# Hybrid encoder block on one core: entry norm with its scalars in PSUM, the triangular inverse in two halves, the mixing shift moved to the project stage

## The chip, the cores and the metric

The kernel runs on 1 core of one Trainium2 chip. The time is the device time of one launch in microseconds (us): the median of three runs. The profile is one further execution, recorded by the hardware profiler. The engines are named as in the profile: PE (matmuls), PEld (its weight loads), DVE (vector), ACT (scalar), POOL (GpSimd), SP (which only issues DMAs here). Each engine works through its own queue in order; an instruction that has to wait holds all behind it on that engine.

## The reference

The input x is 1024 rows (tokens) of 1024 numbers, all in float32. What the changed stages compute:

```python
h = _layer_norm(x, ln_in_w, ln_in_b)            # (x - mean) * rsqrt(var + 1e-5) * w + b, by row
proj = h @ w_in[l]                              # IN_COLS = 1696 (RWKV-7) + 2056 (attention)
...
prev = jnp.pad(p, ((0, 0), (1, 0), (0, 0)))[:, :-1]
p = p + mu * (prev - p)                         # the mixing shift, v is columns 1024 to 1535
...
state = state * wt + sa * bt + vt * kt          # RWKV-7, one step for each token, 8 heads
```

Behind it come the attention of the other 8 heads, the output projection with a norm, a router that picks 4 of 32 experts, the experts (two matrix products with a gated activation between) and a last norm. None of that is touched.

## The kernel before

Tokens are worked in 8 blocks of 128 rows. A product of float32 quality is made of three products of a rounded type: hi x whi, hi x wlo, lo x whi, where hi is the rounded operand and lo what the rounding left.

The stages, in the order of the program:

- **Entry** (the first `with` block of `hybrid_kernel`, lines 161 to 197). For each block: load x, `layer_norm2` (DVE: two `bn_stats`, `bn_aggr`, then the inverse root by three Newton steps on tiles of 128x1 in `rsqrt_steps`, lines 280 to 294; ACT: x times rstd plus a bias, line 318; DVE: times w, line 319; POOL: plus b, line 320). PE turns h (eight transposes, line 182), ACT rounds it to hi (184), DVE takes lo (185), and PE multiplies it by the 512 columns of the v weights in two halves of 24 products each (`ts_mm`, lines 154 to 156). The product v is stored to DRAM (`vraw_d`), read back shifted by one row, mixed with mu by three POOL instructions (194 to 196) and stored as `vp_d`.
- **Project** (`rw_project`): 20 groups of 24 `ws_mm` products of 512 columns on PE for the other RWKV columns, in 4 pairs of heads, each with a long chain on DVE and ACT whose results come back to PE as a few small products (lines 420, 436, 458).
- **Prep** (`rw_prep`) and **attention projections** (`fx_project`), interleaved. `rw_prep` has two loops over 16 chunks of 64 tokens. The first forms the chunk's matrices and keeps their triangular part in `lq`. Then the 16x16 diagonal blocks are inverted: `lq` goes to DRAM (`lq_d`, line 542), comes back with one block per partition and slot (`un`, 544), DVE runs 15 rounds of forward substitution (line 555 four times and line 557 once in each), the result goes to DRAM (`tr_d`, 560) and back (`cmp`, shown as trc, 563). The second loop masks it (577) and completes the inverse with products on PE (583). `fx_project` makes 64 groups of 24 products; each group's result is copied by ACT (476), squared by ACT (479) and summed by DVE (480) in a buffer of which there is one.
- **Scan, attention, output projection, experts, last norm**: unchanged.

Outside the parts that are marked as scheduled by hand, the order on each engine is set when the program is built, by a scheduler that simulates the engines; the program's text sets only what depends on what. So an edit in one stage can move instructions in others. SP issues nearly all loads, in one queue.

Of the kernel before, what the change touches and what calls it, by code (L numbers as in the profile page):

```python
# [74 lines left out]
def hybrid_kernel(ctx: ExitStack, tc: tile.TileContext, A, out):  # L75
# [84 lines left out]
    with tc.tile_pool(name="lnp", bufs=2) as lp:  # L160
        lw = lp.tile([P, D], FT, name="lw", bufs=1)
        lb = lp.tile([P, D], FT, name="lb", bufs=1)
        mub = lp.tile([P, 512], FT, name="mub", bufs=1)
        zr = lp.tile([1, 512], FT, name="zr", bufs=1)
        ve.memset(zr, 0.0)
        sp.dma_start(vraw_d[0:1, :], zr)
        wv = []
        for t in range(NT):
            x = lp.tile([P, D], FT, name="x", bufs=3)
            sp.dma_start(x, A["x"][t * P:(t + 1) * P, :])  # L170
            if t == 0:
# [4 lines left out]
                sp.dma_start(mub, bcast(A["mu_v"], 512))
            h = layer_norm2(nc, lp, x, lw, lb, name="h")
            sp.dma_start(h_d[t * P:(t + 1) * P, :], h)
            for g in range(2):
# [5 lines left out]
                ve.tensor_tensor(lo[dst], ps, f32(hi[dst]), op=OP.subtract)  # L185
            v = lp.tile([P, 512], FT, name="v")
            for j in range(2):
                ps = pa.tile([P, 512], FT, name="mm", bufs=2)[:, :256]
                ts_mm(ps, *wv[j], t)
                ac.copy(v[:, 256 * j:256 * j + 256], ps)  # L190
            sp.dma_start(vraw_d[1 + t * P:1 + (t + 1) * P, :], v)
            d = lp.tile([P, 512], FT, name="vd")
            sp.dma_start(d, vraw_d[t * P:(t + 1) * P, :])
            gp.tensor_tensor(d, d, v, op=OP.subtract)
            gp.tensor_tensor(d, d, mub, op=OP.mult)
            gp.tensor_tensor(d, d, v, op=OP.add)
            sp.dma_start(vp_d[t * P:(t + 1) * P, :], d)

# [1401 lines left out]
```

## Time and profile before

| | |
|---|---|
| Median of 3 runs | 2535.25 us (2532.88 to 2537.62) |
| Profiled execution, its own time | 2537.38 us |
| Span of the profile | 2535.7 us |
| PE busy | 2377.8 us (94%) |
| DVE busy | 1873.3 us (74%) |
| ACT busy | 1323.9 us (52%) |
| POOL busy | 406.8 us (16%) |

A share of busy time is an average over stages with different limits, so the rows below are taken by stage. Times in them are microseconds from the start of the span unless marked ns. Profiled matmuls overlap, so that the start of one to the start of the next, and not the length of one, is the pace.

### The profile page before, as it was taken

How to read it: one execution, taken by the hardware profiler on the slowest of the kernel's cores; microseconds unless marked ns; L12 is line 12 of the kernel's file. 1: busy time of each engine (PE TensorE's matmuls, PEld its weight loads, DVE VectorE, ACT ScalarE, POOL GpSimd, SP SyncE). 2: the span in 40 equal slices, each digit the busy share in tenths (PEclk: the TensorE clock that was granted, in tenths of full speed). 3: DMA queues.
4: the chain of work that ended last, by engine and by line, in shares of the span. 5: the costliest groups of instructions: out<-in, count | busy, mean ns of one | idle time of the engine just before them, and what ended most of it. 6: DMA issues, size and time to landing. Idle time of an engine off the chain costs nothing. (4 is left out here: it accounts for less than half of the span.)

```text
span 2535.7 us, 37299 instructions
## 1 busy us (share of the span) xinstructions
PE 2377.8 (94%) x14105; PEld 1810.4 (71%) x14105; DVE 1873.3 (74%) x2806; ACT 1323.9 (52%) x1610; POOL 406.8 (16%) x370
## 2 busy tenths in 40 slices
PE   5999998989988997789999999999999999999996
PEld 5778998977776765567666767766676676667772
DVE  8367334376887687678878978878897887888884
ACT  2354432364344443346666656666666666566661
POOL 4400211122121111001111101111110111111112
PEclk9999999999999998789999999999999999999998
DMA  6323874127455524569778878977887897788973
GB/s 231 135 74 137 267 228 86 61 80 242 146 191 184 195 76 182 191 208 346 291 281 306 313 299 322 339 292 293 301 332 291 312 336 293 292 302 343 345 291 134
DMA packets 184441, 606.62 MB, mean 239 GB/s; under 512 B 69881, under 2 KB 95609, under 8 KB 130626
## 3 DMA queue, kind: packets, MB, share of 16 engines
q1 hardware_dynamic: 155810, 525.24, 54.6%
q0 software_dynamic: 17456, 65.02, 9.4%
q10 hardware_dynamic: 10992, 13.93, 1.8%
q8 instruction: 113, 1.85, 0.3%
q14 instruction: 70, 0.57, 0.1%
HBM read 518.64 MB, written 85.50 MB: 238 GB/s over the span
## 5 line engine op out<-in xcount | busy, mean ns | idle before, releaser
L1196 DVE TENSOR_TENSOR wl<-raw,wh 128x2048 fp32r<-128x2048 f32 x384 | 873.2, 2288 | 147.0 <-ACT wh L1193 145.9
L1193 ACT CAST wh<-raw 128x2048 fp32r<-128x2048 f32 x381 | 725.9, 1915 | 187.0 <-PE o L1275 67.3
L1219 PE MATMUL h<-wh,xh 128*128 128x512 f32 x1024 | 300.5, 415 | 4.1 <-ACT wh L1193 4.1
L1219 PE MATMUL h<-wl,xh 128*128 128x512 f32 x1024 | 283.0, 398 | 0.2 <-DVE wl L1196 0.2
L1219 PE MATMUL h<-wh,xl 128*128 128x512 f32 x1024 | 281.1, 396 | 0.0
L1219 PEld LDWEIGHTS h<-wl,xh 128*128 128x128 f32 x1024 | 194.2, 190 | 47.8 <-DVE wl L1196 1.0
L1219 PEld LDWEIGHTS h<-wh,xl 128*128 128x128 f32 x1024 | 193.4, 189 | 47.0
L1219 PEld LDWEIGHTS h<-wh,xh 128*128 128x128 f32 x1024 | 184.6, 190 | 42.0 <-ACT wh L1193 4.5
L156 PE MATMUL mm<-whi,hT_lo 128*128 128x256 f32 x640 | 187.3, 294 | 9.5 <-DVE hT_lo L185 5.3
L154 PE MATMUL mm<-whi,hT_hi 128*128 128x256 f32 x640 | 187.7, 294 | 5.5 <-ACT sq L479 3.9
L155 PE MATMUL mm<-wlo,hT_hi 128*128 128x256 f32 x640 | 186.5, 292 | 0.0
L1014 POOL DMA_INDIRECT xg<-h_d,idx x32 | 49.7, 1552 | 777.4 <-PE o L1275 680.5
L1275 PE MATMUL o<-wh,ah 128*128 128x512 f32 x512 | 167.5, 408 | 1.7 <-ACT o L1283 1.7
L1275 PE MATMUL o<-wl,ah 128*128 128x512 f32 x512 | 160.8, 395 | 0.0
L1275 PE MATMUL o<-wh,al 128*128 128x512 f32 x512 | 160.7, 395 | 0.0
L156 PEld LDWEIGHTS mm<-whi,hT_lo 128*128 128x128 f32 x640 | 127.0, 199 | 11.4 <-DVE hT_lo L185 6.5
L154 PEld LDWEIGHTS mm<-whi,hT_hi 128*128 128x128 f32 x640 | 127.0, 198 | 8.8 <-ACT sq L479 4.3
L1213 PE MATMUL ex<-raw,xt 128*32 128x512 f32 x1152 | 132.2, 600 | 0.0
L155 PEld LDWEIGHTS mm<-wlo,hT_hi 128*128 128x128 f32 x640 | 127.1, 199 | 0.0
L1275 PEld LDWEIGHTS o<-wh,ah 128*128 128x128 f32 x512 | 91.0, 188 | 35.2 <-issue 10.9
L1275 PEld LDWEIGHTS o<-wh,al 128*128 128x128 f32 x512 | 96.2, 188 | 23.2
L1275 PEld LDWEIGHTS o<-wl,ah 128*128 128x128 f32 x512 | 96.2, 188 | 23.1
(431 smaller groups left out, 4094.8 us busy)
## 6 DMA issues: line engine op xcount, KB each, us to landing
raw<-w SPq DMA_DIRECT2D x384, 1024.0 KB
pks<-pk_d SPq DMA_DIRECT2D x16, 1152.0 KB
pk_d<-pk POOLq DMA_DIRECT2D x16, 896.0 KB, 5.6
h_d<-h SPq DMA_DIRECT2D x17, 512.0 KB
raw<-w_fx ACTq DMA_DIRECT2D x8, 1024.0 KB
fx_d<-fraw POOLq DMA_DIRECT2D x64, 128.0 KB, 2.8
qkvo<-fx_d SPq DMA_DIRECT2D x32, 256.0 KB
x<-x SPq DMA_DIRECT2D x8, 512.0 KB
```

The lines of the kernel that those rows point to most:

```text
L154: pe.matmul(ps, hi[:, k, n], whi[:, k], start=(k == 0), stop=False)
L155: pe.matmul(ps, hi[:, k, n], wlo[:, k], start=False, stop=False)
L156: pe.matmul(ps, lo[:, k, n], whi[:, k], start=False, stop=(k == KD - 1))
L1014: gp.indirect_dma_start(out=x, out_offset=None, in_=h1_d, in_offset=bass.IndirectOffsetOnAxis(ap=idx[0:m, i:i + 1], axis=0))
L1193: ac.copy(highs[i], raw)
L1196: ve.tensor_tensor(l, raw, f32(h), op=OP.subtract)
L1213: pe.matmul(px[32 * c:32 * c + 32], xt[:, k], raw[:, m], start=False, stop=(k == KD - 1))
L1219: pe.matmul(ps[:, c], x[:, k], w[:, m], start=False, stop=z)
L1275: pe.matmul(po[:, c], x[:, k], w[:, m], start=(k == 0 and x is ah and w is h), stop=z)
```

## The change

Three edits:

1. **Entry.** The order of the entry stage is written out by hand (`tc.manual_schedule()`), with the norm of block t + 2 ahead of the products of block t. The new `layer_norm_in` keeps mean, variance and the two Newton temporaries in PSUM (tile `cps`), drops the last multiplication by -1/8192 and puts that factor into w: a product of a column of -1/8192 with the row w writes w, repeated over 128 partitions, into two PSUM tiles (named qk), and DVE's multiplication by w reads it there, in two halves. POOL's addition of b goes in two halves too. The third load of w, 128 rows from DRAM, is gone; the DVE takes the wlo of the second v weight, which POOL took before.
2. **Mixing shift.** The load of mu, the reading back of v, the three POOL instructions and the store move from the entry into `rw_project`. POOL now loads both v and its shifted rows (two DMAs, line 473 of the new kernel) and stores the result (484), all from its own queue; before, SP issued these DMAs.
3. **Inverse.** `invert(g)` does the inversion for 64 of the 128 partitions, once after chunk 7 and once after chunk 15. All its tiles are set up ahead of the first loop. Each half has 15 rounds with the same number of DVE instructions as the whole had. `un` and `tr_d` are moved in eight DMAs of 8 partitions where each was one.

```diff
 
     def load_w(src, ncols=256, queue=ac, low=ve):
+        raw = fetch_w(src, ncols, queue)
+        return split_w(raw, ncols, low)
+    def fetch_w(src, ncols=256, queue=ac):
         raw = st.tile([P, KD, 256], FT, name="raw")
         queue.dma_start(raw[:, :, :ncols], src)
+        return raw
+    def split_w(raw, ncols=256, low=ve):
         whi = st.tile([P, KD, 256], FR, name="whi")
         wlo = st.tile([P, KD, 256], FR, name="wlo")
...
-        lw = lp.tile([P, D], FT, name="lw", bufs=1)
         lb = lp.tile([P, D], FT, name="lb", bufs=1)
-        mub = lp.tile([P, 512], FT, name="mub", bufs=1)
         zr = lp.tile([1, 512], FT, name="zr", bufs=1)
         ve.memset(zr, 0.0)
-        sp.dma_start(vraw_d[0:1, :], zr)
-        wv = []
-        for t in range(NT):
-            x = lp.tile([P, D], FT, name="x", bufs=3)
-            sp.dma_start(x, A["x"][t * P:(t + 1) * P, :])
-            if t == 0:
-                wv.append(load_w(A["w_v"][0], queue=sp))
-                sp.dma_start(lw, bcast(A["ln_in_w"], D))
-                sp.dma_start(lb, bcast(A["ln_in_b"], D))
-                wv.append(load_w(A["w_v"][1], queue=sp, low=gp))
-                sp.dma_start(mub, bcast(A["mu_v"], 512))
-            h = layer_norm2(nc, lp, x, lw, lb, name="h")
-            sp.dma_start(h_d[t * P:(t + 1) * P, :], h)
+        lrow = lp.tile([1, D], FT, name="lrow", bufs=1)
+        fac = lp.tile([1, P], FT, name="fac", bufs=1)
+        ve.memset(fac, -1.0 / 8192.0)
+        lw = [pq.tile([P, 512], FT, name="qk", bufs=3) for _ in range(2)]
+        cps = pa.tile([P, NT, 8], FT, name="av")
+        xs = []
+        def load_x():
+            t = len(xs)
+            xs.append(lp.tile([P, D], FT, name="x", bufs=4))
+            sp.dma_start(xs[t], A["x"][t * P:(t + 1) * P, :])
+        hs = {}
+        def turn(t):
...
+                hs[t, g] = lambda dst=dst, ps=ps: ve.tensor_tensor(lo[dst], ps, f32(hi[dst]), op=OP.subtract)
+        def low(t):
+            for g in range(2):
+                hs.pop((t, g))()
+        def values(t, j, v):
+            ps = pa.tile([P, 512], FT, name="mm", bufs=2)[:, :256]
+            ts_mm(ps, *wv[j], t)
+            ac.copy(v[:, 256 * j:256 * j + 256], ps)
+        def norm(t):
+            hs[t], r, nm = layer_norm_in(nc, lp, xs[t], cps[:, t])
+            ac.activation(hs[t], xs[t], AF.Identity, bias=nm, scale=r)
+        def weigh(t):
+            h = hs[t]
+            for c in range(2):
+                q = slice(512 * c, 512 * c + 512)
+                ve.tensor_tensor(h[:, q], h[:, q], lw[c], op=OP.mult)
+                gp.tensor_tensor(h[:, q], h[:, q], lb[:, q], op=OP.add)
+            sp.dma_start(h_d[t * P:(t + 1) * P, :], h)
+        with tc.manual_schedule():
+            load_x()
+            sp.dma_start(lrow, A["ln_in_w"][None, :])
+            for c in range(2):
+                pe.matmul(lw[c], fac, lrow[:, 512 * c:512 * c + 512], start=True, stop=True)
+            rv = [fetch_w(A["w_v"][0], queue=sp)]
+            sp.dma_start(lb, bcast(A["ln_in_b"], D))
+            load_x()
+            rv.append(fetch_w(A["w_v"][1], queue=sp))
+            load_x()
+            sp.dma_start(vraw_d[0:1, :], zr)
+            norm(0)
+            weigh(0)
+            wv = [split_w(rv[0])]
+            norm(1)
+            turn(0)
+            low(0)
+            weigh(1)
+            wv.append(split_w(rv[1]))
+            for t in range(NT):
+                if t + 3 < NT:
+                    load_x()
+                if t + 2 < NT:
+                    norm(t + 2)
+                v = lp.tile([P, 512], FT, name="v")
+                values(t, 0, v)
+                if t + 1 < NT:
+                    turn(t + 1)
+                    low(t + 1)
+                if t + 2 < NT:
+                    weigh(t + 2)
+                values(t, 1, v)
+                sp.dma_start(vraw_d[1 + t * P:1 + (t + 1) * P, :], v)
...
+def layer_norm_in(nc, pool, x, ps):
+    ve = nc.vector
+    stt = pool.tile([P, 2, 6], FT, name="ln_st")
+    for c in range(2):
+        ve.bn_stats(stt[:, c], x[:, 512 * c:512 * c + 512])
+    mean, var, a, s = ps[:, 0:1], ps[:, 1:2], ps[:, 2:3], ps[:, 3:4]
+    ve.bn_aggr(ps[:, 0:2], stt)
+    ve.tensor_scalar(a, var, LN_EPS, None, op0=OP.add)
+    r = pool.tile([P, 1], FT, name="ln_r")
+    ve.tensor_scalar(r.bitcast(I32), a.bitcast(I32), -0.5, 1597463007.0, op0=OP.mult, op1=OP.add)
+    for c in (3.0, 12.0, 768.0):
+        ve.scalar_tensor_tensor(s, a, r, r, op0=OP.mult, op1=OP.mult)
+        ve.scalar_tensor_tensor(r, s, c, r, op0=OP.subtract, op1=OP.mult)
+    nm = pool.tile([P, 1], FT, name="ln_nm")
+    ve.scalar_tensor_tensor(nm, mean, -1.0, r, op0=OP.mult, op1=OP.mult)
+    return pool.tile([P, D], FT, name="h", bufs=3), r, nm
...
+        mub = ew.tile([P, 512], FT, name="mub")
+        sp.dma_start(mub, L["bcast"](A["mu_v"], 512))
+        vs = {}
+        def fetch(t):
+            vs[t] = [ew.tile([P, 512], FT, name=n, bufs=2) for n in ("vs", "vd")]
+            for x, o in zip(vs[t], (1, 0)):
+                gp.dma_start(x, vraw_d[o + t * P:o + (t + 1) * P, :])
+        def shift(t):
+            if t == 0:
+                fetch(0)
+            if t + 1 < NT:
+                fetch(t + 1)
+            v, d = vs.pop(t)
+            gp.tensor_tensor(d, d, v, op=OP.subtract)
+            gp.tensor_tensor(d, d, mub, op=OP.mult)
+            gp.tensor_tensor(d, d, v, op=OP.add)
+            gp.dma_start(vp_d[t * P:(t + 1) * P, :], d)
...
             wnext = load_w(A["w_rk"][p + 1] if p + 1 < NP else A["w_fx"][0])
+            for t in (2 * p, 2 * p + 1):
+                shift(t)
...
+    NG = NU // 2
+    def invert(g):
+        p, us = slice(64 * g, 64 * g + 64), slice(NG * g, NG * g + NG)
+        for b in range(8):
+            q = slice(16 * b, 16 * b + 16)
+            o = 16 * (b % 4)
+            sp.dma_start(lq_d[b, us].rearrange("u s t -> s u t"), lq[q, us, o:o + 16])
+        for b in range(8):
+            sp.dma_start(un[64 * g + 8 * b:64 * g + 8 * b + 8].rearrange("p u s t -> p (u s t)"),
+                         lq_d[b, us].rearrange("(x u) s t -> x (u s t)", u=4))
+        T, R = tr[p, :, :, 0], tr[p, :, :, 1]
+        for i in range(1, 16):
+            for u in range(4):
+                ve.tensor_tensor(tm[p, u, :i * i].rearrange("p (k j) -> p k j", j=i), T[:, u, 0:i, 0:i].rearrange("p j k -> p k j"),
+                                 un[p, u, None, 0:i, i].to_broadcast([64, i, i]), op=OP.mult)
+            ve.tensor_reduce(T[:, :, i, 0:i], tm[p, :, :i * i].rearrange("p u (k j) -> p u k j", j=i), axis=AX.X, op=OP.add)
+        for u in range(4):
+            ve.tensor_copy(R[:, u], T[:, u].rearrange("p a b -> p b a"))
+        for b in range(8):
+            sp.dma_start(tr_d[b, us].rearrange("(x u) e -> x (u e)", u=4),
+                         tr[64 * g + 8 * b:64 * g + 8 * b + 8].rearrange("p u a b c -> p (u a b c)"))
+        for b in range(8):
+            sp.dma_start(cmp[16 * b:16 * b + 16, us].rearrange("p u b c -> p u (b c)"), tr_d[b, us].rearrange("u (i e) -> i u e", e=32))
...
-    for b in range(8):
-        q = slice(16 * b, 16 * b + 16)
-        o = 16 * (b % 4)
-        sp.dma_start(lq_d[b].rearrange("u s t -> s u t"), lq[q, :, o:o + 16])
-    un = rw.tile([P, 4, 16, 16], FT, name="un", tag="t0")
-    sp.dma_start(un.rearrange("p u s t -> p (u s t)"), lq_d.rearrange("b (x u) s t -> (b x) (u s t)", u=4))
...
-    for b in range(8):
-        sp.dma_start(cmp[16 * b:16 * b + 16].rearrange("p u b c -> p u (b c)"), tr_d[b].rearrange("u (i e) -> i u e", e=32))
+        if c % (NCH // 2) == NCH // 2 - 1:
+            invert(2 * c // NCH)
```

What moves on DVE in the entry, from the middle of it. Before (lines 286 and 292 are the Newton steps, 310 and 311 the statistics, 319 the product with w; the steps of two blocks are mixed):

```order
L319 TENSOR_TENSOR h<-h,lw 128x1024
L286 SCALAR_TENSOR_TENSOR rq_t<-rq_r,rq_a 128x1
L310 BN_STATS ln_st<-x 128x6
L292 SCALAR_TENSOR_TENSOR rq_r<-rq_t,rq_r 128x1
L311 BN_STATS ln_st<-x 128x6
```

Now (av is the PSUM tile of the scalars, qk the PSUM tile of w):

```order
L380 BN_STATS ln_st<-x 128x6 x2
L382 BN_AGGR av<-ln_st 128x2
L383 TENSOR_SCALAR av<-av 128x1
L385 TENSOR_SCALAR ln_r<-av 128x1
L387 SCALAR_TENSOR_TENSOR av<-av,ln_r 128x1
L388 SCALAR_TENSOR_TENSOR ln_r<-av,ln_r 128x1
...
L390 SCALAR_TENSOR_TENSOR ln_nm<-av,ln_r 128x1
L193 TENSOR_TENSOR hT_lo<-tr,hT_hi 128x4x128 x2
L212 TENSOR_TENSOR h<-h,qk 128x512 x2
```

Each block's norm, lo of the block before it and product with w now stand in this fixed sequence (the pair of lines 387 and 388 stands three times in it). The operands of the Newton steps that were both in SBUF are one in SBUF and one in PSUM.

What moves on SP at the end of the first loop of `rw_prep` (bbd, kbd and ar are a chunk's loads; lq_d, un, tr_d, trc as above). Before:

```order
L518 DMA bbd_1810<-bh_d 64x4x64 x2
L515 DMA ar<-ar_d 128x4x128
L519 DMA kbd_1814<-kh_d 64x4x64 x2
L542 DMA lq_d<-lq 16x64x16 x8
L544 DMA un<-lq_d 128x1024
L560 DMA tr_d<-tri 128x2048
```

Now:

```order
L646 DMA ar<-ar_d 128x4x128
L650 DMA kbd_1824<-kh_d 64x4x64 x2
L625 DMA lq_d<-lq 16x32x16 x4
L638 DMA tr_d<-tri 8x2048 x8
L625 DMA lq_d<-lq 16x32x16 x4
L641 DMA trc<-tr_d 16x32x32 x7
L627 DMA un<-lq_d 8x1024
L641 DMA trc<-tr_d 16x32x32
L627 DMA un<-lq_d 8x1024 x7
```

The stores and loads of the first half's result (lines 638 and 641) now stand between the second half's lq_d and its un. The first half's own lq_d and un stand among the loads of chunks 9 to 11.

What moves on POOL (vs and vd are v and its shifted rows, lb the bias b of the norm). Before, in the entry:

```order
L320 TENSOR_TENSOR h<-h,lb 128x1024
L194 TENSOR_TENSOR vd<-vd,v 128x512
L195 TENSOR_TENSOR vd<-vd,mub 128x512
L196 TENSOR_TENSOR vd<-vd,v 128x512
L320 TENSOR_TENSOR h<-h,lb 128x1024
```

Now, from the entry's end on:

```order
L213 TENSOR_TENSOR h<-h,lb 128x512 x16
L473 DMA vs<-vraw_d 128x512
L473 DMA vd<-vraw_d 128x512
L473 DMA vs<-vraw_d 128x512
L473 DMA vd<-vraw_d 128x512
L481 TENSOR_TENSOR vd<-vd,vs 128x512
L482 TENSOR_TENSOR vd<-vd,mub 128x512
L483 TENSOR_TENSOR vd<-vd,vs 128x512
L484 DMA vp_d<-vd 128x512
```

The entry keeps only the additions of b on POOL; all eight shifts follow them in one run, each with the loads of the next block ahead of it and no other POOL work between.

## Rows read from the trace of the kernel before

**Rows 1.** Windows: stretch, its length, then PE, PEld, DVE, ACT, POOL busy (instructions), clock, DMA.

```profile
0.00:95.00 95.00, 65.68 (x450) 61.59 (x451) 63.78 (x141) 30.20 (x45) 49.95 (x34) 0.95 0.56 199
95.00:228.00 133.00, 131.62 (x556) 95.25 (x554) 86.17 (x89) 60.94 (x67) 6.93 (x5) 1.00 0.29 107
260.00:512.00 252.00, 237.31 (x1980) 236.36 (x1980) 91.89 (x213) 85.10 (x232) 44.21 (x82) 0.97 0.52 156
```

**Rows 2.** Waits of PE, 0 to 95 us: waiter, releaser, total, times, longest.

```profile
PE tr L182 <- POOL h L320: 17.6, 2, 16.1
PE mm L156 <- DVE rq_a L280: 4.2, 2, 3.7
```

**Rows 3.** Waits of PE, 228 to 512 us.

```profile
PE qk L583 <- DVE t L577: 8.1, 1, 8.1
PE mm L154 <- ACT sq L479: 3.9, 2, 3.1
```

**Rows 4.** Groups, DVE and ACT, 0 to 95 us: busy, mean ns, idle before.

```profile
L286 DVE SCALAR_TENSOR_TENSOR rq_t<-rq_r,rq_a 128x1 f32<-128x1 f32 x24 | 18.8, 792 | 0.4
L137 DVE TENSOR_TENSOR wlo<-raw,whi 128x2048 fp32r<-128x2048 f32 (+1 forms) x2 | 4.6, 2301 | 6.3 <-ACT whi L136 6.3
L318 ACT ACTIVATE h<-x,ln_nm,rq_r 128x1024 f32<-128x1024 f32 x8 | 9.9, 1247 | 11.1 <-DVE ln_nm L316 11.1
```

**Rows 5.** Timeline of POOL and of DVE in the entry: start, length.

```profile
58.32 2.38 POOL L320 TENSOR_TENSOR h<-h,lb 128x1024 f32<-128x1024 f32 x1 [4.51 <-issue]
72.59 1.28 POOL L195 TENSOR_TENSOR vd<-vd,mub 128x512 f32<-128x512 f32 x1
...
58.28 2.42 DVE L286 SCALAR_TENSOR_TENSOR rq_t<-rq_r,rq_a 128x1 f32<-128x1 f32 x1
73.18 1.29 DVE L185 TENSOR_TENSOR hT_lo<-tr,hT_hi 128x512 fp32r<-128x512 f32 x2 [4.46 <-ACT hT_hi L184]
```

**Rows 6.** Timeline of the first block's norm, and PE's first product.

```profile
5.67 0.69 DVE L310 BATCH_NORM_STATS2 ln_st<-x 128x6 f32<-128x512 f32 x1 [2.90 <-DMA x<-x]
...
9.15 0.16 DVE L316 SCALAR_TENSOR_TENSOR ln_nm<-ln_mv,rq_r 128x1 f32<-128x1 f32 x1
...
17.88 0.58 PE L154 MATMUL mm<-whi,hT_hi 128*128 128x256 f32 x1
```

**Rows 7.** Timeline of DVE in the last norm, whose tile ch lies in PSUM.

```profile
2521.90 0.17 DVE L1496 TENSOR_TENSOR ch<-ch,frr 128x2 f32<-128x2 f32 x1
2522.10 0.17 DVE L1498 TENSOR_TENSOR ch<-ch,frr 128x2 f32<-128x2 f32 x1
```

**Rows 8.** Timeline: PE at two blocks' first products, ACT at a rounding and the entry's end.

```profile
65.83 0.39 PE L154 MATMUL mm<-whi,hT_hi 128*128 128x256 f32 x1 [0.24 <-ACT hT_hi L184]
73.20 0.39 PE L154 MATMUL mm<-whi,hT_hi 128*128 128x256 f32 x1 [0.24 <-ACT hT_hi L184]
...
72.56 1.08 ACT L184 CAST hT_hi<-tr 128x512 fp32r<-128x512 f32 x2
...
94.52 0.37 ACT L190 COPY v<-mm 128x256 f32<-128x256 f32 x1
```

**Rows 9.** Timeline of one pair in project: DVE's last result, PE's use of it.

```profile
169.56 1.28 DVE L455 SCALAR_TENSOR_TENSOR sh<-sh,cv,sh 128x1024 f32<-128x1024 f32 x1
...
175.12 1.95 PE L458 MATMUL av<-bdones,sh 128*128 128x2 f32 x16
```

**Rows 10.** Timeline of the inverse: SP's two runs of eight DMAs, DVE's steps.

```profile
353.47 12.05 SPq L542 DMA_DIRECT2D lq_d<-lq  x8
404.35 9.79 SPq L563 DMA_DIRECT2D trc<-tr_d  x8
...
372.97 0.37 DVE L555 TENSOR_TENSOR trt<-tri,un 128x1 f32<-128x1 f32 x4 [7.65 <-DMA un<-lq_d]
398.56 1.30 DVE L559 COPY tri<-tri 128x256 f32<-128x256 f32 x4
419.92 0.69 DVE L577 TENSOR_TENSOR t<-trc,bm 128x512 f32<-128x512 f32 x1 [11.31 <-DMA trc<-tr_d]
```

More of the change, by code (lines that the diff above doesn't have):

```diff
@@ L181, in hybrid_kernel @@
                 for j in range(4):
-                    pe.transpose(ps[:, j], h[:, (4 * g + j) * P:(4 * g + j + 1) * P], ident)
+                    pe.transpose(ps[:, j], hs[t][:, (4 * g + j) * P:(4 * g + j + 1) * P], ident)
                 dst = (slice(None), slice(4 * g, 4 * g + 4), slice(t * P, (t + 1) * P))
                 ac.copy(hi[dst], ps)
[L185 to L197, printed above, removed]
+                hs[t, g] = lambda dst=dst, ps=ps: ve.tensor_tensor(lo[dst], ps, f32(hi[dst]), op=OP.subtract)
@@ L487, in rw_prep @@
     ar_d, bh_d, kh_d, lq_d, tr_d, pk_d = (L[k] for k in ("ar_d", "bh_d", "kh_d", "lq_d", "tr_d", "pk_d"))
+    vraw_d, vp_d = L["vraw_d"], L["vp_d"]
     H = (slice(0, 64), slice(64, 128))
@@ L510, in rw_prep @@
     lq = rw.tile([P, NU, CH], FT, name="lq")
+    un = rw.tile([P, 4, 16, 16], FT, name="un", tag="t0")
+    tr = rw.tile([P, 4, 16, 2, 16], FT, name="tri")
+    gp.memset(tr, 0.0)
+    tm = rw.tile([P, 4, 225], FT, name="trt")
+    one = rw.tile([P, 64], FT, name="one")
+    gp.memset(one, 1.0)
+    diag = bass.AP(tensor=tr.tensor, offset=tr.offset, ap=[list(tr.ap[0]), [512, 4], [33, 16]])
+    gp.tensor_copy(diag, one.rearrange("p (u i) -> p u i", u=4))
+    cmp = rw.tile([P, NU, 2, 16], FT, name="trc")
+    NG = NU // 2
[21 more added lines that the diff above has]
+            sp.dma_start(cmp[16 * b:16 * b + 16, us].rearrange("p u b c -> p u (b c)"), tr_d[b, us].rearrange("u (i e) -> i u e", e=32))
     for c in range(NCH):
@@ L536, in rw_prep @@
         gp.dma_start(pk_d[c][:, 0:PK1], pk)
-    for b in range(8):
-        q = slice(16 * b, 16 * b + 16)
-        o = 16 * (b % 4)
-        sp.dma_start(lq_d[b].rearrange("u s t -> s u t"), lq[q, :, o:o + 16])
-    un = rw.tile([P, 4, 16, 16], FT, name="un", tag="t0")
-    sp.dma_start(un.rearrange("p u s t -> p (u s t)"), lq_d.rearrange("b (x u) s t -> (b x) (u s t)", u=4))
-    tr = rw.tile([P, 4, 16, 2, 16], FT, name="tri")
-    gp.memset(tr, 0.0)
-    tm = rw.tile([P, 4, 225], FT, name="trt")
-    T, R = tr[:, :, :, 0], tr[:, :, :, 1]
-    one = rw.tile([P, 64], FT, name="one")
-    gp.memset(one, 1.0)
-    diag = bass.AP(tensor=tr.tensor, offset=tr.offset, ap=[list(tr.ap[0]), [512, 4], [33, 16]])
-    gp.tensor_copy(diag, one.rearrange("p (u i) -> p u i", u=4))
-    for i in range(1, 16):
-        for u in range(4):
-            ve.tensor_tensor(tm[:, u, :i * i].rearrange("p (k j) -> p k j", j=i), T[:, u, 0:i, 0:i].rearrange("p j k -> p k j"),
-                             un[:, u, None, 0:i, i].to_broadcast([P, i, i]), op=OP.mult)
-        ve.tensor_reduce(T[:, :, i, 0:i], tm[:, :, :i * i].rearrange("p u (k j) -> p u k j", j=i), axis=AX.X, op=OP.add)
-    for u in range(4):
-        ve.tensor_copy(R[:, u], T[:, u].rearrange("p a b -> p b a"))
-    sp.dma_start(tr_d.rearrange("b (x u) e -> (b x) (u e)", u=4), tr.rearrange("p u a b c -> p (u a b c)"))
-    cmp = rw.tile([P, NU, 2, 16], FT, name="trc")
-    for b in range(8):
-        sp.dma_start(cmp[16 * b:16 * b + 16].rearrange("p u b c -> p u (b c)"), tr_d[b].rearrange("u (i e) -> i u e", e=32))
+        if c % (NCH // 2) == NCH // 2 - 1:
+            invert(2 * c // NCH)
     for c in range(NCH):
```

## The prediction

> **What bounds the kernel now.** I read the windows by stage first [rows 1]. From 95 to 228 us (project) PE is busy 131.6 of 133 us, from 260 to 512 us (prep and attention projections) 237.3 of 252; in the first 95 us (entry) it is busy 65.7. So the stages that the change touches are bound by PE, and what can be won is the time in which PE waits. In those rows the reader is to see PE's share and that DVE has room in the later two stages: 86.2 of 133 us and 91.9 of 252.
>
> Next the waits of PE. In the entry it waits 16.1 us for the first h, up to 3.7 us at a time for DVE's small norm steps, and so on [rows 2]. From 228 to 512 us the waits on the inverse are 8.1 us for the first mask (line 577, which waits for trc) and 3.9 us for the square on ACT (line 479) [rows 3]: 12.0 us. The second has its cause on DVE, where un came 7.65 us late [rows 10] and held the sums (line 480) that stood behind it.
>
> Last the group of DVE's Newton steps [rows 4]: line 286 takes 792 ns on average, 24 times. The timeline shows why: at 58.28 us such a step takes 2.42 us and ends with POOL's addition of b, which runs from 58.32 for 2.38 us; yet lo, one operand of which is in PSUM, runs at 73.18 us at its usual 1.29 us for a pair while POOL works from 72.59 to 73.87 [rows 5]. Small steps with both tensors in SBUF are held by POOL; with one in PSUM DVE isn't held.
>
> **Part 1, the entry.** Removed: 24 steps of line 286 at 0.79 us instead of 0.2 us, 14.2 us of held DVE; eight multiplications; a load of 512 KB ahead of the second x. Added: two PE products at the start, nothing waits behind them.
>
> What bounds then? By the written order a loop runs through DVE and ACT, one block a turn: norm of t + 2 on DVE, ACT's scaling, ACT's copy of v, ACT's rounding of block t + 1, lo of it on DVE, product with w on DVE. Norm: 5.67 to 9.31 us now, 3.64 [rows 6], less one step of 0.2, is 3.45. ACT: 1.25 [rows 4], 0.37 [rows 8], and 0.62 from the rounding's start (72.56) [rows 8] to lo's (73.18) [rows 5]. DVE: lo 1.29 [rows 5], the product with w at the same size and again one operand in PSUM, an estimate of 1.29. Sum 8.27 us. PE needs 7.37 a block (65.83 to 73.20) [rows 8], so the loop sets the pace, 0.9 above PE's.
>
> That the norm's steps cost no more with PSUM operands I take from the last norm, where such steps stand 0.20 us apart [rows 7]. The Trainium skill speaks against it (VectorE: DVE Perf Modes, the section on the TRN2 errata): its cycle table has 120 cycles of fixed cost from PSUM where SBUF has 58. By that table ten small steps would cost an estimated 0.65 us more a block and the entry would gain 4 us less. The rows of this case decide.
>
> The start, from x's arrival as now (5.67): norm 3.45, ACT 1.25, w 1.29, wlo 2.30 [rows 4], norm of block 1 3.45, ACT 1.25 and 0.62: the first product at 19.3 us, or 20.6 if wlo (both operands in SBUF) is held by one POOL step of 1.28 [rows 5]. That is later than now (17.88) [rows 6]. Block 1: lo 1.29, w 1.29, wlo 2.30 and up to 1.3 of hold, norm 3.45, ACT 2.24: 29.9 to 32.5, middle 31.2. Five turns of 8.27 bring block 6 to 72.6; blocks 6 and 7 have no norm ahead and run at PE's pace, 7.37 and, without transposes behind, about 6.1: 86.1. Now the last product ends at 94.5 [rows 8]. Entry: **-8.4 us**. Best end: every block at 7.37, 81.5, so -13. Worst end: steps held as now, 14.2 / 8 = 1.8 us more a turn, 95.1, so +1.
>
> **Part 2, the shift.** It leaves the entry, where it is one cause of the held steps (counted above), and adds to project 24 POOL steps of 1.28 us [rows 5], 30.7 us, beside a DVE that is busy 86 of 133 us and often reads two SBUF operands. POOL is free there (6.9 us busy) [rows 1], so the steps run from the entry's end on without waiting for a pair. PE uses a pair's last result 4.3 us after DVE ends it (170.84 to 175.12) [rows 9], so a delay of one or two POOL steps is covered. I take 0. A gain is excluded, since PE has 1.4 us of idle time there in all; the loss is bounded by DVE's 30.7 us of holding, without that cover. What waits behind POOL's DMAs on its queue is only the next shift, and vp_d is read first in the scan.
>
> **Part 3, the inverse.** Now it takes 66.5 us from the first lq_d (353.47) to the mask (419.92) [rows 10], against the attention products that PE has meanwhile. In the new order the first half starts after chunk 7 of 16, half a loop earlier, and the second loop needs only that half: its 8.1 us go. DVE's work doubles: 372.97 to 399.86 is 26.9 us with a few other steps in it, once more, in a stage with 160 us of idle DVE.
>
> What is late next is the second half. SP now has eight tr_d and seven trc of the first half between the second half's lq_d and its un, and they wait for the first half's rounds. From the end of the copies (399.86) to trc's landing is 20.1 us now; with half the bytes and un behind it I put 10 to 20 us. DVE reaches the second half's first step four sums after the first loop, four groups of 24 products or about 12 us (a block of 48 and eight transposes takes 7.37). So DVE may wait up to 8 us with the sums behind it, as it does now for 7.65 us, and PE pays at the same place, the square of line 479: I take 6 us, with 0 and 10 as bounds. I add 2 us (0 to 6) for what the first half does in the first loop: its lq_d and un are issued among the loads of chunks 9 to 11, and its rounds stand between the masks of six chunks. Together -12.0 + 6 + 2 = **-4 us**, bounds -12 and +4.
>
> **Sum.** 2537.38 - 8.4 + 0 - 4 = 2525.0 us for an execution like the profiled one. The median of the runs is 2.1 us lower, so 2522.9, say **2523 us**. Downstream, PE's sequence is the same from the early part of the attention on (about its row 2800 of 6830); before that some rows change places, for which I allow 3 us either way. Time won early is kept, since nothing later waits for a fixed moment.
>
> **Rivals.**
> - *The stalls only change place* (PSUM steps dearer, the wait of the second half at its 10 us): entry -5, prep 0, about 2530. For it: the loop of 8.27 already is DVE's, and the same SP queue feeds the second half. Against: the steps in PSUM [rows 7].
> - *The inverse gets in the way of the first loop:* lq_d took 12.05 us of SP [rows 10]; if half of that, the un behind it and DVE's rounds between the masks hold the chunks by 12 us, the prep loses 8 instead of gaining 4: 2535, no change. For it: PE has no spare products at that place unless the new order puts them there, which it does by a few.
> - *Slower, the shift against DVE in project:* each POOL step holds a DVE step with two SBUF operands, and PE, in order, waits for the chains. It decides once DVE is late by more than the 4.3 us of cover. The Trainium skill has this as a rule (SBUF — State Buffer, the section on its two sides): the pair of ports that DVE and GpSimd share is locked for a whole instruction, and the other engine stands still. The trace agrees in the entry, with 2.42 us for a small step. Price: 30.7 less the cover once, 26.4 us; 2523 + 26 = 2549. Against: 46.8 us of idle DVE there, and that the first shifts fall in project's light beginning.
>
> **Chances.** Forecast 0.55 (own range 2516 to 2530), stalls that move 0.2, the inverse in the way 0.15, the shift against DVE 0.1. Faster by over 0.2% (5 us, about what a measurement can tell here): all of the first, half of the second and a little of the third, 0.68; within 0.2%: 0.2; slower: 0.12. Range 2513 to 2538: down to both parts near their best ends, up to the third case.
>
> **What would show it.** In the entry, the Newton steps near 0.2 us each while POOL works, and products of blocks 2 to 6 starting about 8.3 us apart; the last product near 86 us. In project, PE idle below 3 us. In prep, no wait of line 583's first product on the mask, and one wait of 5 or so us behind the square, with DVE held on the second un. I am wrong if the Newton steps stay long, if project's PE idle grows past 10 us, or if PE waits in the first loop of the prep for its chunks' loads or masks by more than 6 us.

## The result and the profile after

The changed kernel takes 2521.33 us (median of 5 runs, 2518.18 to 2525.85); the kernel before took 2537.62 us (2532.88 to 2540.21) beside it. The ratio is 0.9939, 95% interval 0.9928 to 0.9951. Forecast were 2523 us and a profiled execution 12.4 us shorter; the spans are 2535.7 and 2519.6 us, so 16.1 us were won. The total is close; its terms are not. Executions of one and the same kernel differ by about 7 us (above), and every stage below is read from one execution, so a few microseconds in a stage that an edit doesn't touch prove nothing by themselves.

To see where the time went I marked four points in both traces: the start of the last copy of the values (end of the entry), of the last copy into bon, a small tile that closes a pair (end of project), of the last product of the second prep loop, and the end of the span.

| stage (us of the profiled execution) | before | after | change | forecast |
|---|---|---|---|---|
| entry, to 94.5 / 85.9 | 94.5 | 85.9 | -8.6 | -8.4 |
| project, to 259.5 / 259.1 | 165.0 | 173.2 | +8.2 | 0 |
| prep loops and attention products, to 584.1 / 573.9 | 324.6 | 314.8 | -9.8 | -4 |
| all the rest | 1951.6 | 1945.7 | -5.9 | 0, 3 either way |

The windows of the changed kernel by these stages (columns: stretch, its length, busy time of PE, PEld, DVE, ACT, POOL with instructions, granted clock, DMA share, GB/s):

```profile
0.00:86.00 86.00, 64.91 (x454) 57.51 (x454) 53.23 (x143) 28.40 (x44) 25.42 (x22) 1.00 0.51 174
86.00:259.00 173.00, 168.16 (x809) 128.98 (x808) 121.35 (x117) 77.06 (x95) 60.26 (x63) 0.97 0.40 143
259.00:574.00 315.00, 300.06 (x2509) 290.68 (x2508) 168.26 (x425) 125.98 (x349) 60.36 (x109) 0.99 0.48 144
574.00:2519.00 1945.00, 1841.18 (x10344) 1325.64 (x10342) 1551.85 (x2204) 1087.58 (x1123) 279.85 (x208) 0.98 0.73 269
```

And of the kernel before, its last two stages:

```profile
259.00:584.00 325.00, 303.04 (x2514) 294.59 (x2513) 147.44 (x349) 126.09 (x349) 61.37 (x110) 0.98 0.46 139
584.00:2535.00 1951.00, 1846.49 (x10342) 1328.96 (x10341) 1551.17 (x2202) 1090.92 (x1123) 280.83 (x208) 0.97 0.73 268
```

Length less PE's busy time is what PE waits: from the project's end to the second loop's end 22.0 us before and 14.9 after. Its busy time fell too, by 3.0 us for the same work (2514 and 2509 instructions), and in the rest by 5.3 us: there the granted clock differs, 0.97 against 0.98. Project went the other way, as the next views show. First PE's waits from 86 us to the second loop's end (total, times, longest):

```profile
PE mm L161 <- ACT sq L573: 6.9, 2, 6.5
PE mm L154 <- ACT rk L495: 2.7, 1, 2.7
PE qk L530 <- ACT kn L525: 2.2, 1, 2.2
```

The mask's 8.1 us [rows 3] are gone, the square's (3.9 before) has grown to 6.9, with 6 forecast, and project has two waits that it did not have. The timeline of project, engine by engine, shows their cause (start, length, line; vd is the shift's tile, kn and sh are a pair's tiles):

```profile
131.46 1.28 POOL L481 TENSOR_TENSOR vd<-vd,vs 128x512 f32<-128x512 f32 x1
133.53 1.30 POOL L482 TENSOR_TENSOR vd<-vd,mub 128x512 f32<-128x512 f32 x1
134.91 3.17 POOL L483 TENSOR_TENSOR vd<-vd,vs 128x512 f32<-128x512 f32 x1
...
142.47 2.52 POOL L483 TENSOR_TENSOR vd<-vd,vs 128x512 f32<-128x512 f32 x1
...
146.39 1.30 POOL L481 TENSOR_TENSOR vd<-vd,vs 128x512 f32<-128x512 f32 x1
...
133.34 3.65 DVE L517 TENSOR_TENSOR_SCAN cs<-seg,cs 128x1024 f32<-128x1024 bf16 x1
...
143.76 2.31 DVE L502 TENSOR_TENSOR sh<-rk 128x1024 f32<-128x1024 f32 x1
146.10 2.68 DVE L503 SCALAR_TENSOR_TENSOR sh<-sh,cv,rk 128x1024 f32<-128x1024 f32 x1
...
137.08 1.06 ACT L520 ACTIVATE wt<-cs 128x1024 f32<-128x1024 f32 x1 [6.81 <-DVE cs L517]
...
140.78 0.58 ACT L495 COPY rk<-mm 128x512 f32<-128x512 f32 x1
...
148.81 1.15 ACT L525 ACTIVATE kn<-sh,cv 128x1024 f32<-128x1024 f32 x1 [3.99 <-DVE sh L503]
...
141.42 0.50 PE L154 MATMUL mm<-hT_hi,whi 128*128 128x512 f32 x1 [2.66 <-ACT rk L495]
...
150.02 1.37 PE L530 MATMUL qk<-kn,bdones 128*128 128x512 f32 x2 [2.17 <-ACT kn L525]
```

Beside each of POOL's steps stands a step of DVE that takes about that much longer. The scan of line 517 takes 3.65 us, and without the shift's arithmetic 2.29 (run e6 below); ACT's wt waits for it, ACT's copy of rk stands behind wt on its queue, and PE waits 2.66 us for rk. DVE's step of line 503 takes 2.68 us and that of line 502 2.31, and in e6 1.28 and 1.22; ACT's kn waits for them, and PE waits 2.17 us for kn. PE was not only idle in project. Later in it, with PE busy without a gap since 150.02, eight products start about 0.43 us apart and then again 0.23 apart, the lower and the upper of the two clock levels (1.2 and 2.4 GHz). Just before stand 16 products of two columns each (line 552); the first and last of the eight and their neighbours:

```profile
171.57 1.95 PE L552 MATMUL av<-bdones,sh 128*128 128x2 f32 x16
...
174.39 0.39 PE L154 MATMUL mm<-hT_hi,whi 128*128 128x512 f32 x1
174.62 0.58 PE L155 MATMUL mm<-hT_lo,whi 128*128 128x512 f32 x1
175.00 0.63 PE L156 MATMUL mm<-hT_hi,wlo 128*128 128x512 f32 x1
175.43 0.63 PE L154 MATMUL mm<-hT_hi,whi 128*128 128x512 f32 x1
...
177.56 0.63 PE L156 MATMUL mm<-hT_hi,wlo 128*128 128x512 f32 x1
177.99 0.44 PE L154 MATMUL mm<-hT_hi,whi 128*128 128x512 f32 x1
178.27 0.39 PE L155 MATMUL mm<-hT_lo,whi 128*128 128x512 f32 x1
```

In the entry the Newton steps are short, with line 387 where line 286 stood [rows 4]:

```profile
L387 DVE SCALAR_TENSOR_TENSOR av<-av,ln_r 128x1 f32<-128x1 f32 x24 | 5.4, 227 | 0.9
L388 DVE SCALAR_TENSOR_TENSOR ln_r<-av,ln_r 128x1 f32<-128x1 f32 x24 | 3.8, 157 | 0.8
```

### The profile page after: what moved, and what is told of

It is laid out like the page before. It is cut to its first block, busy times and chain, and to the rows that moved or that the text cites. A ratio compares the mean times of both kernels' runs of the same rounds, so it can differ in the third digit from the quotient of the medians.

```text
span 2519.6 us, 37444 instructions
## 1 busy us (share of the span) xinstructions
PE 2374.3 (94%) x14109; PEld 1802.8 (72%) x14109; DVE 1894.7 (75%) x2887; ACT 1319.0 (52%) x1610; POOL 425.9 (17%) x401
```

## The experiments

Each was timed in 5 rounds beside the kernel before. All profiled executions by the same four stages, one execution a kernel:

| run | entry | project | loops | rest | span | median | ratio to before, interval |
|---|---|---|---|---|---|---|---|
| changed kernel | 85.9 | 173.2 | 314.8 | 1945.7 | 2519.6 | 2521.3 | 0.9939, 0.9928 to 0.9951 |
| e1 | 104.1 | 168.9 | 320.4 | 1965.0 | 2558.4 | 2561.0 | 1.0101, 1.0088 to 1.0114 |
| e5 | 103.9 | 175.3 | 312.3 | 1958.3 | 2549.8 | 2551.1 | 1.0050, 1.0037 to 1.0063 |
| e6 | 86.4 | 164.6 | 316.0 | 1948.0 | 2515.0 | 2515.1 | 0.9915, 0.9901 to 0.9929 |
| e4 | 85.7 | 171.8 | 310.5 | 1956.9 | 2524.9 | 2526.3 | 0.9961, 0.9949 to 0.9973 |
| e8 | 86.7 | 164.8 | 311.0 | 1951.7 | 2514.2 | 2518.5 | 0.9919, 0.9904 to 0.9935 |
| e9 | 86.2 | 166.1 | 313.6 | 1954.2 | 2520.1 | 2520.8 | 0.9927, 0.9914 to 0.9941 |
| e12 | 86.2 | 172.1 | 321.4 | 1956.5 | 2536.2 | 2534.3 | 0.9980, 0.9971 to 0.9989 |
| e13 | 81.0 | 167.1 | 328.2 | 1958.9 | 2535.2 | 2533.2 | 0.9973, 0.9959 to 0.9986 |
| e3 | 85.8 | 168.6 | 323.6 | 1951.0 | 2529.0 | 2532.6 | 0.9981, 0.9971 to 0.9990 |
| e14 | 81.3 | 166.6 | 316.1 | 1954.4 | 2518.4 | 2519.5 | 0.9924, 0.9910 to 0.9938 |
| e17 | 86.5 | 163.3 | 309.7 | 1957.4 | 2516.9 | 2520.2 | 0.9932, 0.9916 to 0.9948 |
| e18 | 81.5 | 164.7 | 311.7 | 1954.3 | 2512.2 | 2514.9 | 0.9910, 0.9891 to 0.9930 |

In e6, e8 and e18 PE executes the same rows in the same order as in the changed kernel; in the others the scheduler also moved later rows.

**e6, the shift without its arithmetic.**

```
-            gp.tensor_tensor(d, d, v, op=OP.subtract)
-            gp.tensor_tensor(d, d, mub, op=OP.mult)
-            gp.tensor_tensor(d, d, v, op=OP.add)
```

> The changed kernel without the three GpSimd steps of the shift in project (vd is loaded and stored as it is, so the shift is left out of the computation); the order on the other engines is the same. Theory 1 (these 24 steps hold DVE, and the late chains cost project 8 to 9 us between its first and last product: 4.8 us of waits and the rest half-speed stretches): the waits on rk and kn go, the granted clock is 1.00 in the whole of project, 2521.3 - 8 = 2513 us. Theory 2 (the loss comes from the loads and stores on GpSimd's queue or from the new order of rows): within 1.5 us of 2521.

Measured 2515.1 us; project 164.6 instead of 173.2. Its row:

```profile
86.00:251.00 165.00, 164.99 (x813) 127.49 (x813) 109.15 (x118) 77.28 (x95) 20.40 (x39) 0.99 0.43 149
```

PE doesn't wait at all. Against the changed kernel's row of project, PE waited 4.8 us there and was busy 3.2 us longer on the same work; DVE was busy 12.2 us longer, POOL 39.9 us for steps that alone would be 24 times 1.28 us. Theory 1 holds for the 8 us: the kernels with POOL's steps in project take 168.6 (e3) to 173.2 us there, those without 163.3 to 167.1 (e1 and e5 left out, whose late entry reaches into project). At the end of the span 4.6 us are left, by the medians 6.2, and the two intervals just meet. One part of theory 1 misses: the clock is not 1.00 throughout. Without any wait, PE falls to the lower level here too, behind the same 16 products of two columns:

```profile
164.97 2.21 PE L549 MATMUL av<-bdones,sh 128*128 128x2 f32 x16
...
168.05 0.63 PE L155 MATMUL mm<-hT_lo,whi 128*128 128x512 f32 x1
168.47 0.63 PE L156 MATMUL mm<-hT_hi,wlo 128*128 128x512 f32 x1
```

**e1 and e5, the shift put back into the entry, its load on GpSimd's queue; e5 with the norm in SBUF besides.**

```
+            gp.dma_start(d, vraw_d[t * P:(t + 1) * P, :])
+            gp.tensor_tensor(d, d, v, op=OP.subtract)   # both: of the block before
...
-        cps = pa.tile([P, NT, 8], FT, name="av")         # e5 alone
+        cps = lp.tile([P, NT, 8], FT, name="cps", bufs=1)
```

> The values' shift is put back into the entry loop (three GpSimd steps a block, of the block before, loads and stores from GpSimd's queue); the norm stays in PSUM and the inverse in two halves. Theory 1 (GpSimd holds only DVE steps with all operands in SBUF; in the entry those are few, in project many): the turns of the entry stay at 8.0 to 8.5 us, its last values copy comes within 1.5 us of 85.9, project loses its 4.8 us of waits on ACT and runs at a granted clock of 1.00 throughout, so 2521.3 - 8 + 1 = 2514 us. Theory 2 (GpSimd's own time counts: b's additions then stand behind the shift, 25 + 31 = 56 of 86 us busy): the turns grow to 9 us or more, the entry gives back what project wins, 2520 to 2523 us.

> The kernel with the shift in the entry, and the norm's small tensors (mean, variance, a, s) in SBUF instead of PSUM; nothing else differs. Theory 1 (where the operands lie decides): the Newton steps (with the product r*r and the difference) go from 0.23 and 0.16 us to about 0.8 and 0.36 as before the change, some 13 to 18 us of held DVE in all, 1.5 to 2 us a turn, and the time is 8 to 14 us above that kernel's: about 2525. Theory 2 (the steps are short since GpSimd has less to do, or does it at other moments): both kernels agree within 2 us.

Both miss in time, under either theory: 2561 and 2551 us, e5 10 us below e1 and not above it. POOL stood in its queue for each load, and b's addition, which PE's transposes need, stood behind it:

```profile
61.22 1.29 POOL L192 TENSOR_TENSOR vd<-vd,v 128x512 f32<-128x512 f32 x1 [5.04 <-DMA vd<-vraw_d]
...
66.11 2.48 POOL L224 TENSOR_TENSOR h<-h,lb 128x512 f32<-128x512 f32 x2
...
127.21 0.06 DVE L450 MEMSET t<- 104x1 f32 x1 [16.41 <-POOL vd L193]
```

The entry took 104 us, and project's first tile waited until POOL's last block was done (last row), probably since it takes over that memory. What the pair does settle is where the operands lie. In e1 (PSUM) the steps keep 227 and 157 ns through all this. In e5 (SBUF) they average 336 and 386 ns, and three of them take 2.78 to 2.91 us; POOL's pair of one such moment, and the step between its neighbours:

```profile
66.23 2.49 POOL L224 TENSOR_TENSOR h<-h,lb 128x512 f32<-128x512 f32 x2
...
65.58 0.22 DVE L402 SCALAR_TENSOR_TENSOR cps<-cps,ln_r 128x1 f32<-128x1 f32 x1
65.83 2.91 DVE L403 SCALAR_TENSOR_TENSOR ln_r<-cps,ln_r 128x1 f32<-128x1 f32 x1
68.78 0.22 DVE L402 SCALAR_TENSOR_TENSOR cps<-cps,ln_r 128x1 f32<-128x1 f32 x1
```

The same step in e1:

```profile
66.01 0.16 DVE L403 SCALAR_TENSOR_TENSOR ln_r<-av,ln_r 128x1 f32<-128x1 f32 x1
```

The held step of e5 ends with b's pair on POOL, 66.23 to 68.72 us. It had begun 0.4 us ahead of the pair, while POOL was issuing its store, and so did the other two, 0.25 and 0.33 us ahead. In e1 the steps at 66.01 and 66.20 stand beside e1's pair (66.11, above) and take 0.16 us. That e5 is yet 10 us faster comes after project, where its rows stand in another order.

**e8, the shift in the entry with its loads on SP, its arithmetic two blocks late.**

```
+            if t > 1:
+                shift(t - 2)                  # three GpSimd steps, behind b's addition
...
+            if t:
+                fetch_d(t - 1)                # sp.dma_start(vd, vraw_d[...])
```

> The shift in the entry once more, with its loads on SP, issued a turn after the store that they read, and its three GpSimd steps behind b's addition of the same turn, for the block two turns back; its tiles lie where project doesn't need them. TensorE's and ScalarE's order is the changed kernel's. Theory 1 (GpSimd's steps cost only where DVE has SBUF-only steps behind which TensorE waits): turns of 8.0 to 8.5 us, last values copy at 85.9 to 87.4, project without its waits and ending 8 us earlier, 2514 to 2517 us. Theory 2 (the shift takes GpSimd's time from b's addition, 6.5 us of steps a turn and about 1 us of issue): turns of 9 us or more, 2521 us or more.

Theory 1 holds in the stages: entry 86.7, project 164.8, no wait of PE in project. The time, 2518.5 us, lies 1.5 us above its range, and the interval (0.9904 to 0.9935) meets that of the changed kernel. The whole shift is hidden in the entry; what stopped e1 was the load on POOL's own queue and its timing (e8 moved both, the load to SP and the steps one block later).

**e9, the shift's steps on DVE.** Edit: `ve.tensor_tensor` for `gp.tensor_tensor` in the three lines.

> The shift stays in project, but its 24 steps run on DVE instead of GpSimd (one engine name changed in three lines; some 210 rows of TensorE in project change place). From the norm's DVE step of 128x1024 in SBUF before the change (1.25 us) a step of half the size is an estimated 0.63 us, so 15 us of DVE's own time in place of 31 us in which GpSimd can hold it. Theory 1: half of the 8.1 us that project lost comes back, the waits on rk and kn are below 2.5 us together: 2517 us. Theory 2 (DVE stands in its queue for the shift's loads, or the chains are late just the same): 2521 us or more.

Measured 2520.8 us. A step takes 0.69 us, 16.5 us in all; DVE stands 12.8 us for the loads, PE still 3.2 us for rk. Project wins 7.1 us back, and the rest is 8.5 us longer; neither theory has that. Its row of project shows waits without any loss of clock, with PE busy 162.9 us, less than in e6:

```profile
86.20:252.30 166.10, 162.92 (x810) 125.69 (x809) 122.88 (x142) 77.05 (x95) 20.35 (x39) 1.00 0.42 149
```

**e12, the norm in SBUF; e13, the norm in PSUM and nothing else of the change.**

```
-        cps = pa.tile([P, NT, 8], FT, name="av")          # e12
+        cps = lp.tile([P, NT, 8], FT, name="cps", bufs=1)
...
-            h = layer_norm2(nc, lp, x, lw, lb, name="h")  # e13, in the kernel before
+            h = layer_norm_ps(nc, lp, x, lw, lb, cps[:, t])
```

> The changed kernel with the norm's small tensors in SBUF instead of PSUM (the shift stays in project). Theory 1 (the prediction's: PSUM is what frees the Newton steps): with SBUF operands they are held by b's additions, 1 us or more a turn, and the last values copy comes at 92 us or later. Theory 2 (with the shift out of the entry, b's additions fall beside bn_stats and beside steps with a PSUM operand, and nothing is left that could hold the Newton steps): turns of 8.0 to 8.5 us, last values copy at 85 to 87.5. The order of later rows changes too, so only the entry is compared.

> The kernel before, with the norm's mean, variance, a and s in PSUM and nothing else of the change (the shift stays on GpSimd in the entry, its loads on SP). Theory 1 (the prediction's): the Newton steps fall from 0.79 and 0.36 to 0.23 and 0.16 us although GpSimd works as before, some 18 us less on DVE, and the last values copy comes at 86 to 89 instead of 94.5: 2529 to 2532 us. Theory 2 (the steps are short, but the entry is paced by GpSimd's additions and SP's queue): the copy comes at 92 or later, 2535 to 2538 us.

In e12 the entry ends at 86.2 with steps of 232 and 159 ns: theory 2. With the shift gone and the order by hand, b's pair falls beside the statistics, and no Newton step takes more than 0.32 us. In e13 theory 1 holds for the entry and more: 225 and 153 ns although POOL works as before, and the last copy at 81.0 us, 13.5 us earlier. Yet e13 is 0.27% faster only, 2533.2 us, between the two theories: 7.8 of the 13.5 us are left at the end of the second loop (576.3), none at the experts' first product (1036.2 before, 1036.4 now). And e12 is 10 us (by the ratios) to 13 us (by the medians) slower than the changed kernel with the same entry, and the intervals do not meet: rows from the end of project on stand in another order, and each later stage but project is longer.

**e3, one inverse; e14, e13 with the inverse in two halves.**

```
-        if c % (NCH // 2) == NCH // 2 - 1:     # e3; e14 adds it to e13
-            invert(2 * c // NCH)
```

> The changed kernel with the inverse in one piece after the first loop, as before (entry and shift as changed; rows from the middle of project's end on change place). Theory 1 (the two halves are worth what the prep's waits show: 8.1 and 3.9 us gone, 6.9 come): the wait on the first mask is back with 8 us or more, the second loop's last product comes 7 to 9 us later than in the changed kernel, counted from the entry's last copy, 2528 to 2531 us. Theory 2 (the prep's gain came from rows that only changed place): 2519 to 2523 us.

> The kernel before with two things: the norm's small tensors in PSUM (as in the run that did this alone, whose entry ended at 81.0 us) and the inverse in two halves; entry order left to the scheduler, shift on GpSimd in the entry. Theory 1 (what is won early stays if the later order is as good as the changed kernel's): entry's last copy at 81, project without waits, the second loop's last product 5 us ahead of the kernel with the shift in the entry and its loads on SP, 2507 to 2512 us. Theory 2 (the order that the scheduler gives the later rows costs more than the entry wins, as when the norm alone was moved): 2519 us or more.

e3: 2532.6 us, the mask's wait is back with 6.7 us, the loops take 8.8 us more: theory 1, with the time 1.6 us above its range (its project is 4.6 us shorter, with a wait of 0.5 us for kn instead of 2.2). e13 and e14 have the same entry and project within 0.5 us each, and the loops take 328.2 and 316.1: 12.1 us for the two halves. e14 is no better than e8: 2519.5 us, theory 2's time. In the profiled executions its loops and its rest are 5.1 and 2.7 us longer than e8's; whether the order of the rows does that is not shown.

**e4 and e17, the second half's un ahead of the first half's tr_d and trc**, in the changed kernel and in e8.

```
         if c == NCH - 1:
             fetch_un(1)                # lq_d and un of the second half
             hand_on(0)                 # tr_d and trc of the first
...
```

SP's rows in the changed kernel show what the second un stands behind, and DVE's row what that costs:

```profile
358.58 4.82 SPq L638 DMA_DIRECT2D tr_d<-tri  x8
363.44 4.32 SPq L625 DMA_DIRECT2D lq_d<-lq  x4
367.80 3.83 SPq L641 DMA_DIRECT2D trc<-tr_d  x7
371.67 0.38 SPq L627 DMA_DIRECT2D un<-lq_d  x1
372.09 0.30 SPq L641 DMA_DIRECT2D trc<-tr_d  x1
372.44 4.29 SPq L627 DMA_DIRECT2D un<-lq_d  x7
...
379.30 0.38 DVE L632 TENSOR_TENSOR trt<-tri,un 64x1 f32<-64x1 f32 x4 [10.26 <-DMA un<-lq_d]
```

> The second half's lq_d and un are issued on SP ahead of the first half's tr_d and trc (only the place in the program of these calls is changed; the scheduler moves some rows after it). Theory 1 (the second un waits for some 8.7 us of issues on SP: eight tr_d 4.82, seven trc 3.83): un lands 5 to 8 us earlier, DVE's wait of 10.3 us for it shrinks below 5, PE's 6.5 us behind the square goes, and no mask is waited for: 2521.3 - 6 = 2515 us. Theory 2 (the stall only moves: trc of the first half now comes late for the first mask of the second loop, or the chain of the second half ends late for chunk 8): a wait of 4 us or more on the mask or on trc, 2520 to 2523 us.

> The kernel with the shift in the entry (loads on SP), with the second half's un issued ahead of the first half's tr_d and trc. It has TensorE's order of the run that made this edit to the changed kernel, where the second loop ended 5.9 us earlier and the execution 5.3 us later. Theory 1 (the new order of TensorE's rows after the prep costs those 11 us): again the second loop ends about 5 us earlier, and the time is 4 to 6 us above that of the kernel without this edit, 2520 to 2524 us. Theory 2 (the loss came from where the half-speed stretches happened to fall): at or below it, 2509 to 2518 us.

e4: the loops are 4.3 us shorter, DVE's wait before the second half's first step is 6.1 us instead of 10.3 and the square's wait 3.3, no mask waits, and still it takes 2526.3 us, which neither theory has; the rest is 11.2 us longer. e17: loops 1.3 us shorter than e8's, the rest 5.7 longer, 2520.2 us. With the same order of PE in both, the rest is 1956.9 and 1957.4 us. That speaks for theory 1 of e17, that the order of the later rows costs more than the un wins, but does not show it: e17 lies 1.7 us above e8 and not 4 to 6, and the intervals of e17 and e8, and of e4 and the changed kernel, meet.

**e18, e8 with ScalarE's casts ahead of its scaling.**

```
-                if t + 2 < NT:
+                if t + 2 < NT and not (t < 5):
                     norm(t + 2)
...
                 if t + 1 < NT:
                     turn(t + 1)
+                if t + 2 < NT and (t < 5):
+                    norm(t + 2)
```

> The kernel with the shift in the entry (loads on SP), with one thing moved in its written order: in the first five turns ScalarE's rounding of block t+1 is ahead of its scaling of block t+2, instead of behind it. The rows of all other engines keep their order to the end of the program. Theory 1 (the loop of 8.0 us a turn is one of order: DVE waits 2.1 us a turn for the rounding, which stands behind the scaling): turns fall to TensorE's 7.4, the last values copy comes at 82 to 83.5 instead of 86.7, and the later stages keep it: 2514 to 2516 us, against 2518.5. Theory 2 (time won here is lost again where half-speed stretches and the serial stages of later rows fall otherwise): the copy comes at 82 to 83.5, but the time is 2517 us or more.

ACT's rows of one turn in the changed kernel, where the casts (line 192) stand behind the scaling (line 206):

```profile
45.44 1.24 ACT L206 ACTIVATE h<-x,ln_nm,ln_r 128x1024 f32<-128x1024 f32 x1 [5.23 <-DVE ln_nm L390]
46.59 0.35 ACT L202 COPY v<-mm 128x256 f32<-128x256 f32 x1
46.84 1.07 ACT L192 CAST hT_hi<-tr 128x512 fp32r<-128x512 f32 x2
```

and in e18:

```profile
48.69 1.07 ACT L207 CAST hT_hi<-tr 128x512 fp32r<-128x512 f32 x2
51.20 1.24 ACT L221 ACTIVATE h<-x,ln_nm,ln_r 128x1024 f32<-128x1024 f32 x1 [1.44 <-POOL vd L193]
```

Theory 1: the last copy at 81.5 us, 2514.9 us, the lowest median of all. Its interval (0.9891 to 0.9930) still meets that of the changed kernel (0.9928 to 0.9951), so the gain over it is likely, not certain; that over e8, whose interval covers most of it, is not shown.

## Why the prediction came out right

Right in total by luck: project lost 8.2 us that the forecast put at nothing, the loops won 5.8 us more than forecast, and the rest, which had no term, gave 5.9 us.

**Part 1: right in size, its cause only half.** The forecast was -8.4, measured -8.6, by the steps that it named: the first norm 3.49 us, the last copy at 85.9 (86.1), turns of 8.0 where x was there in time (8.27). That operands in PSUM free the steps is shown (e5 against e1, and e13). But e12 shows that in the changed kernel the PSUM places do nothing for the entry: with the shift out and the order by hand it ends within 0.3 us without them. So these edits do not add up. The order by hand alone is not enough, since e5 has it too and its steps are held; the shift's move alone was not run. PSUM costs a step nothing, as the forecast took it: 227 ns stand against 232 with all in SBUF (e12). The Trainium skill (VectorE: DVE Perf Modes, the section on the TRN2 errata) would have it cost 62 cycles more a step, and the 4 us estimated from that are not there. The hold itself shows in e5: a step of 0.16 us took 2.91 and ended with POOL's pair. This agrees with the Trainium skill's rule (SBUF — State Buffer, the section on its two sides) that one of the two engines stands still for the other's whole instruction. And the 8.0 us loop is an effect of the written order: with ACT's casts first the entry ends at 81.5, the forecast's own best end. The scheduler's own order does as well: with the PSUM tiles and nothing else it ends at 81.0 (e13), 4.9 us ahead of the changed kernel.

**Part 2: the step that failed.** "A delay of one or two POOL steps is covered. I take 0." It cost 8.2 us (e6: 8.6). The cover of 4.3 us was read at one place, and the holds were taken one or two at a time. From 131 to 149 us four steps in a chain are held, 2.06 and 3.65 us, then 2.31 and 2.68, where e6 has 0.69, 2.29, 1.22 and 1.28 on average: 5.2 us. With the steps just before and between them DVE ends line 503 at 148.78, where e6 ends it at 140.18: 8.6 us late, beyond the cover. The rival on the shift had mechanism and place right and the price wrong: of 30.7 us of POOL steps DVE was held for 12.2, and PE waited for 4.8. The bound that I set, PE idle above 10 us, would not have caught it, since 3.2 us more were lost at the lower clock. (e9 had 3.2 us of waits in project and lost nothing to the clock, so these 3.2 us do not follow from the waits alone.)

**Part 3: the right steps, under-sized.** The sum was -12.0 + 6 + 2 = -4. The two removed waits went and the new one of 6.9 came, as forecast. The 2 us in the first loop did not appear; one wait of the kernel before, at the first loop's start, was gone instead:

```profile
PE qk L524 <- issue: 2.8, 1, 2.8
```

It is back with 2.5 us in e6, whose project is short, but also with 2.3 in e4, whose project is long, so what takes it away is not shown. The loops became 9.8 us shorter, 8.8 against e3 and 12.1 from e13 to e14. By the windows PE waited 7.0 us less and was busy 3.0 us less on the same rows. The waits that the forecast named make -5.1 of these 7.0 (8.1 and 3.9 gone, 6.9 come).

**The rest had no term.** "Time won early is kept, since nothing later waits for a fixed moment", with 3 us allowed either way. It was -5.9 us, nearly all in PE's busy time (5.3), with a granted clock of 0.98 against 0.97. In the four kernels with one and the same order of PE (changed kernel, e6, e8, e18) it is 1945.7, 1948.0, 1951.7 and 1954.3 us, the changed kernel's the shortest, though these kernels differ only ahead of it. And executions of one kernel differ as much: the changed kernel took 2518.18 us at a mean granted clock of 0.981 and 2525.85 at 0.976. So that the change caused the 5.9 us is not shown. With another order of the rows the rest reaches 1965.0 us (e1). So e6 wins 8.6 us in project and keeps 4.6, and e13 keeps 0.5 of 13.5 in its profiled execution. In project every fall of the clock, in all fourteen kernels, stands in or close behind a wait of PE, or in or within 2 us behind one of the four sets of 16 products of two columns. But only 13 of these 56 sets have one, and none of the waits in e9 and e14, so what decides where the clock falls stays open.

## What to carry to other kernels

Price a step that runs on GpSimd not by its own length but by the chain on VectorE that it can hold, each held step once, and look for the engine that waits behind that chain; then put it where VectorE's steps read PSUM, and its loads on another queue than its arithmetic. Where a stage is bound by TensorE, read its waits and its busy time apart: here 4.8 us of waits came with 3.2 us at the lower clock, but in e9 3.2 us of waits came with none, so a wait has no fixed price. When a scheduler orders the rows, compare stage by stage, and hold its order fixed in the experiment: two kernels with the same entry and another order of later rows (e12 and the changed one) differ by more than the entry's edit won. And time several executions: one kernel's own differ by 7 us.

## What the hardware showed that was not expected

TensorE fell to its lower clock in work without a gap: from 174.62 to 177.99 us its products start 0.43 us apart, having run 0.23 apart, and it had been busy since 150.02. What it did just before was 16 products of two columns, for 1.95 us. The same stands ahead of the fall in e6, where PE does not wait in project at all. In the kernel before, the same products stand in project [rows 9], and the granted clock is 1.00 from 95 to 228 us [rows 1] and on to the stage's end.

A GpSimd step beside VectorE's SBUF steps is itself lengthened: 24 steps of 1.28 us took 39.9 us in project, 3.17 us for one of them, which began at 134.91 beside the scan of line 517 and ended 1.1 us after it.
